# The chain of an RWKV scan on Trainium2: a second PSUM bank, products split by their output columns, one output addition, and I - X added in PSUM

## The chip, the cores and the metric

The kernel runs on one core of a Trainium2 chip. Its five engines work through instruction lists of their own, each in order: TensorE (PE, with the loads of its stationary operand shown apart as PEld), VectorE (DVE), ScalarE (ACT), GpSimd (POOL) and SyncE (SP, which issues the DMAs). They wait for each other through semaphores. The metric is the time of one execution on the device in microseconds (us); lower is better.

## The reference

The reference is one layer of a hybrid encoder on 1024 + 256 tokens of width 1024. The normalised input is projected to three branches, neighbourhood attention, a bidirectional RWKV-7 recurrence and attention to a memory; their gated outputs are merged, and a convolutional feed-forward layer follows. The change is in the recurrence, which has 8 heads of width 64 and runs once forward and once backward:

```
def step(s, inp):
    r_t, w_t, k_t, v_t, a_t, b_t = inp
    sa = einsum('bhij,bhj->bhi', s, a_t)
    s = s * w_t[:, :, None, :] + sa[..., None] * b_t[:, :, None, :] + v_t[..., None] * k_t[:, :, None, :]
    return s, einsum('bhij,bhj->bhi', s, r_t)
```

## The kernel before

The recurrence is computed in chunks of 64 tokens. One item of work is a pair of heads (p, 4 of them), a direction (d, 2) and a block of 256 tokens, that is 4 chunks (s, 5): 40 items and 160 chunks in all. `part_rwkv` goes through them, alternating the directions.

For each item `rw_prepare` (L538 on) makes what doesn't depend on the state. From loaded blocks it computes decays with small products into the tile `ps_l` (L558, L559), ScalarE, GpSimd and VectorE work, Gram products (`ps_gE` L608, `ps_gO` L611), masks (L618 to L623) and transposes (`ps_bt` L628, L631). Then it inverts a 128 x 128 triangular matrix per chunk: five levels of two products each (L653, L658) with copies on ScalarE (L655, L660), an addition and a transpose on VectorE (L661, L664) and masked copies on GpSimd (L650). The inverse X is refined once: L672 forms I - X on VectorE, L675 and L676 compute the product of the matrix (in two fp16 halves) with X, L678 adds both on VectorE, L681 multiplies by X again and L683 adds, which gives TT.

`rw_chain` carries the state from chunk to chunk. R holds, for each chunk and each of the two heads h, the state in 64 of its 128 partitions and the values V in the other 64. Per chunk: two products with L1 (L707, one for each head, 128 columns out of 128 partitions), a copy Q of both (L709, ScalarE), one product with TT (L710), two half copies back into R (L719 ScalarE, L720 VectorE), two products with L3 (L722), two additions that make the next chunk's state (L731, L732, VectorE) and two that make the output Ys (L733, L734, VectorE). GpSimd scales the state in between (L715, L717). All products of a chunk write one PSUM tile `ps_c`, of which there is one buffer.

TensorE is kept busy by other work: after each prepare and each chain `fill` puts in steps of the dense products of attention and gates (`ps_d`, L205), a fixed number per item. The written order is a request only: a scheduler at build time lays out every engine's list by priority and by its own estimate of costs, and the PSUM and SBUF buffers that are free in that estimate. The engines then follow these lists. PSUM has eight banks; a tile in one bank isn't written by TensorE and read by another engine at the same time, so accesses to one tile are ordered even where they touch different columns.

A matrix product has a shape of the array: 128 rows by 128 columns by default, 64*128 where the contraction is over 64 partitions (L608, L611, L628), 128*64 or 64*64 where it makes 64 output partitions. The profile shows it before the operand's shape. An fp32 product appears as two records.

Of the kernel before, what the change touches and what calls it, by code (L numbers as in the profile page):

```python
# [77 lines left out]
def make_consts():  # L78

    c = {}  # L80
    c["ident"] = np.eye(128, dtype=np.float32)
    c["ident16"] = np.eye(128, dtype=np.float16)
    hb = np.arange(128) // 64
    c["headones"] = (hb[:, None] == hb[None, :]).astype(np.float32)
# [70 lines left out]
class Builder:  # L155
# [195 lines left out]
    def rwkv_consts(self):  # L351
# [14 lines left out]
        self.reset = ld("reset", [128, 256])  # L366
        self.ident16 = ld("ident16", [128, 128], F16)
        d0 = ld("rw_decay0", [128, 2, 4])
        a0 = ld("rw_a0", [128, 2, 4])
# [134 lines left out]
    def part_rwkv(self):  # L504
        nc, tc = self.nc, self.tc
        with ExitStack() as cx:
            pool = cx.enter_context(self.pool("rw", 2))
            self.psg = cx.enter_context(self.pool("psg", 2, space=PSUM))
            self.psl = cx.enter_context(self.pool("psl", 1, space=PSUM))
            self.psi = cx.enter_context(self.pool("psi", 1, space=PSUM))  # L510
            self.psc = cx.enter_context(self.pool("psc", 1, space=PSUM))
            self.L1 = [pool.tile([128, 4, 2, 128], F32, name="L1_%d" % i, bufs=1) for i in range(3)]
# [25 lines left out]
    def rw_prepare(self, pool, p, d, s):  # L538
# [17 lines left out]
        nc.sync.dma_start(lw[dl], self.LW[s][dl])  # L556
        ps = self.psl.tile([128, 512], F32, tag="l", name="ps_l")
        nc.tensor.matmul(ps[:, 0:256], lhsT=self.decay2[dl, pc], rhs=lw[dl, 0], start=True, stop=True)  # L558
# [89 lines left out]
        for l in range(1, 6):  # L648
# [21 lines left out]
            X, XT = X2, XT2  # L670
        IX = tl([128, 4, 128], "IX", F16, bufs=1)
        nc.vector.tensor_sub(IX, bc(self.ident16), X)  # L672
        pe = self.psi.tile([128, 4, 128], F32, tag="i%d" % (i % 2), name="ps_e")
        for c in range(4):
            nc.tensor.matmul(pe[:, c, :], lhsT=Lh[:, c, :], rhs=X[:, c, :], start=True, stop=False)  # L675
            nc.tensor.matmul(pe[:, c, :], lhsT=Ll[:, c, :], rhs=X[:, c, :], start=False, stop=True)  # L676
        Er = IX
        nc.vector.tensor_add(f(Er), f(IX), f(pe))  # L678
        pe = self.psi.tile([128, 4, 128], F32, tag="i%d" % (i % 2), name="ps_n")
# [6 lines left out]
    def rw_chain(self, pool, it, state):  # L686
# [9 lines left out]
        for n, c in enumerate(order):  # L696
            if n == 0:
                if first:
                    nc.gpsimd.memset(R[0:64, c, 0, :], 0.0)
                    nc.gpsimd.memset(R[64:128, c, 1, :], 0.0)  # L700
                else:
                    S = state.pop((p, d))
                    nc.scalar.copy(R[0:64, c, 0, :], S[0:64])
                    nc.vector.tensor_copy(R[64:128, c, 1, :], S[64:128])
            ps = self.psc.tile([128, 3, 2, 64], F32, tag="c", name="ps_c")
            for h in range(2):
                nc.tensor.matmul(ps[:, 0, h, :], lhsT=L1[:, c, h, :], rhs=R[:, c, h, :], start=True, stop=True)  # L707
            Q = pool.tile([128, 2, 64], F32, tag="Q", name="Q", bufs=4)
            nc.scalar.copy(Q, ps[:, 0])  # L709
            nc.tensor.matmul(ps[:, 1].rearrange("p h i -> p (h i)"), lhsT=TT[:, c, :],  # L710
                             rhs=Q.rearrange("p h i -> p (h i)"), start=True, stop=True)
            more = n < 3 or not last
            if more:
                SW = pool.tile([128, 64], F32, tag="SW", name="SW", bufs=2)
                nc.gpsimd.tensor_scalar(SW[0:64], R[0:64, c, 0, :], scalar1=wC[0:64, c:c + 1], scalar2=1.0,  # L715
                                        op0=ALU.mult, op1=ALU.mult)
                nc.gpsimd.tensor_scalar(SW[64:128], R[64:128, c, 1, :], scalar1=wC[64:128, c:c + 1], scalar2=1.0,  # L717
                                        op0=ALU.mult, op1=ALU.mult)
            nc.scalar.copy(R[0:64, c, 0, :], ps[0:64, 1, 0, :])  # L719
            nc.vector.tensor_copy(R[64:128, c, 1, :], ps[64:128, 1, 1, :])  # L720
            for h in range(2):
                nc.tensor.matmul(ps[:, 2, h, :], lhsT=L3[:, c, h, :], rhs=R[:, c, h, :], start=True, stop=True)  # L722
            if more:
                if n < 3:
                    nx = R[:, order[n + 1]]
                    o0, o1 = nx[0:64, 0, :], nx[64:128, 1, :]
                else:
                    S = pool.tile([128, 64], F32, tag="S%d" % d, name="S", bufs=2)
                    o0, o1 = S[0:64], S[64:128]
                    state[(p, d)] = S  # L730
                nc.vector.tensor_add(o0, SW[0:64], ps[0:64, 2, 0, :])  # L731
                nc.vector.tensor_add(o1, SW[64:128], ps[64:128, 2, 1, :])  # L732
            nc.vector.tensor_add(Ys[64:128, c, :], Q[64:128, 0, :], ps[64:128, 2, 0, :])  # L733
            nc.vector.tensor_add(Ys[0:64, c, :], Q[0:64, 1, :], ps[0:64, 2, 1, :])  # L734
        nc.sync.dma_start(self.Y[d][p][:, 4 * s:4 * s + 4], Ys)
# [962 lines left out]
```

## Time and profile before

| | |
|---|---|
| runs, median (3) | 3095.74 us (3078.0 to 3098.25) |
| profiled execution | 3087.64 us |
| its span | 3085.9 us |
| mean granted clock of TensorE | 0.967 |
| the RWKV stage, first chain product to last | 391 to 1416 us of the span |

The span is the stretch between the first and the last instruction of the profiled execution; its own time is 1.7 us longer. The page divides the span into 40 slices; the RWKV stage is roughly slices 6 to 18. Busy times of TensorE include the time in which a product runs through the array, so a busy TensorE can still have room: how far apart the starts of successive records are says more.

### The profile page before, as it was taken

How to read it: one execution, taken by the hardware profiler on the slowest of the kernel's cores; microseconds unless marked ns; L12 is line 12 of the kernel's file. 1: busy time of each engine (PE TensorE's matmuls, PEld its weight loads, DVE VectorE, ACT ScalarE, POOL GpSimd, SP SyncE). 2: the span in 40 equal slices, each digit the busy share in tenths (PEclk: the TensorE clock that was granted, in tenths of full speed). 3: DMA queues.
4: the chain of work that ended last, by engine and by line, in shares of the span. 5: the costliest groups of instructions: out<-in, count | busy, mean ns of one | idle time of the engine just before them, and what ended most of it. 6: DMA issues, size and time to landing. Idle time of an engine off the chain costs nothing.

```text
span 3085.9 us, 49265 instructions
## 1 busy us (share of the span) xinstructions
PE 2929.3 (95%) x18164; PEld 2477.7 (80%) x18164; DVE 1946.3 (63%) x4001; ACT 1242.3 (40%) x2693; POOL 1082.5 (35%) x1186
## 2 busy tenths in 40 slices
PE   7999989999999998999989999999899999999999
PEld 6878867767777777777877788898799999997877
DVE  6233387887887888883435551474688888883233
ACT  6322344444444544552545551022244344343232
POOL 2000166765666766662122100000245544441100
PEclk9999988997999999999979999999999999999999
DMA  6332412221222222214546534544112222245343
GB/s 229 119 120 94 137 62 67 73 78 61 76 74 70 86 64 66 66 54 132 167 123 192 178 114 157 191 163 147 66 61 71 75 77 68 68 135 165 131 146 103
DMA packets 212743, 333.51 MB, mean 108 GB/s; under 512 B 45282, under 2 KB 109538, under 8 KB 212502
## 3 DMA queue, kind: packets, MB, share of 16 engines
q1 hardware_dynamic: 211062, 325.12, 32.6%
q10 hardware_dynamic: 1440, 5.24, 0.4%
q8 instruction: 143, 2.34, 0.3%
q14 instruction: 98, 0.80, 0.1%
HBM read 230.15 MB, written 104.07 MB: 108 GB/s over the span
## 4 chain that ended last, share of the span: by engine, by line
PE 75%; DVE 10%; POOL 6%; issue 3%; ACT 3%; DMA 2%; SPq 0%; ACTq 0%; POOLq 0%; DVEq 0%
PE ps_d L205 26%; PE ps_d L1470 16%; PE ps_d L1660 9%; PE ps_w L1167 3%; PE ps_o L945 3%; PE ps_c L722 2%; PE ps_c L707 2%; PE ps_y L653 1%; PE ps_gO L611 1%; PE ps_pt L863 1%; PE ps_x L658 1%; DVE X L661 1%; PE ps_gE L608 1%; PE ps_c L710 1%; PE ps_bt L628 1%
## 5 line engine op out<-in xcount | busy, mean ns | idle before, releaser
L205 PE MATMUL ps_d<-hT,whi 128*128 128x512 f32 (+1 forms) x2688 | 689.3, 381 | 3.5 <-ACT gt L824 2.9
L205 PEld LDWEIGHTS ps_d<-hT,whi 128*128 128x128 f32 x2688 | 450.5, 194 | 65.6 <-issue 5.8
L205 PE MATMUL ps_d<-hT,wlo 128*128 128x512 f32 (+1 forms) x1344 | 358.2, 383 | 0.0
L650 POOL TENSOR_TENSOR Lk<-Lh,c_lev 128x512 f16<-128x512 f16 x200 | 242.2, 1214 | 128.2 <-PE ps_y L653 127.0
L1660 PE MATMUL ps_d<-hT,h2T 128*128 128x512 f32 x1110 | 275.4, 394 | 7.3 <-POOL hT L183 4.1
L1660 PEld LDWEIGHTS ps_d<-hT,h2T 128*128 128x128 f32 x1110 | 210.5, 190 | 54.5 <-POOL hT L183 5.3
L205 PEld LDWEIGHTS ps_d<-hT,wlo 128*128 128x128 f32 x1344 | 229.6, 197 | 29.0 <-issue 2.8
L183 DVE TENSOR_TENSOR wlo<-wraw,whi 128x512 fp32r<-128x512 f32 x152 | 117.1, 781 | 192.9 <-ACT whi L182 192.0
L1374 DVE SCALAR_TENSOR_TENSOR xk<-xk,fconv,xk 128x642 f32<-128x642 f32 (+1 forms) x176 | 178.7, 1026 | 3.1
L655 ACT CAST Yl<-ps_y 128x512 f16<-128x512 f32 x200 | 116.8, 584 | 135.6 <-PE ps_y L653 134.8
L1470 PE MATMUL ps_d<-hT,fwx 128*128 128x256 f32 (+1 forms) x1080 | 159.0, 306 | 2.2 <-ACT fwx L182 1.6
L1470 PEld LDWEIGHTS ps_d<-hT,fwx 128*128 128x128 f32 x1080 | 156.5, 188 | 2.9 <-ACT fwx L182 1.9
L660 ACT CAST X<-ps_x 128x512 f16<-128x512 f32 x200 | 116.7, 584 | 101.7 <-PE ps_x L658 95.2
L1470 PE MATMUL ps_d<-hT,fw 128*128 128x256 f32 (+1 forms) x1032 | 156.1, 310 | 0.6 <-ACT hT L182 0.6
L1340 DVE TENSOR_TENSOR xk<-ps_d,xk 128x256 f32<-128x256 f32 (+1 forms) x308 | 140.6, 480 | 22.1 <-PE ps_d L1470 21.8
L1470 PEld LDWEIGHTS ps_d<-hT,fw 128*128 128x128 f32 x1032 | 153.2, 190 | 1.6 <-ACT hT L182 0.9
L1219 POOL TENSOR_TENSOR xk<-xk 128x1536 f32<-128x1536 f32 (+1 forms) x2 | 5.8, 2918 | 387.2 <-DVE xk L1157 387.2
L182 ACT CAST whi<-wraw 128x512 fp32r<-128x512 f32 x152 | 91.3, 620 | 119.9 <-PE ps_d L205 104.8
L205 PE MATMUL ps_d<-bo,whi 128*128 128x256 f32 (+2 forms) x640 | 127.0, 337 | 4.2 <-DMA bo<-O 3.1
L1383 ACT ACTIVATE xk<-xk 128x320 f32<-128x320 f32 (+1 forms) x88 | 41.7, 474 | 214.9 <-DVE xk L1387 139.8
L707 PEld LDWEIGHTS ps_c<-R,L 128*128 128x128 f32 x640 | 92.0, 201 | 43.2 <-issue 24.8
L1470 PE MATMUL ps_d<-h2T,fw 128*128 128x384 f32 (+1 forms) x840 | 125.4, 308 | 0.0
(353 smaller groups left out, 6437.6 us busy)
## 6 DMA issues: line engine op xcount, KB each, us to landing
wraw<-in_w_in SPq DMA_DIRECT2D x112, 256.0 KB, 2.9
wraw<-in_w_up SPq DMA_DIRECT2D x88, 256.0 KB, 2.6
kr<-RKV SPq DMA_DIRECT2D x40, 384.0 KB, 3.2
bo<-O SPq DMA_DIRECT2D x24, 640.0 KB, 8.7
gate<-GT SPq DMA_DIRECT2D x20, 640.0 KB, 4.0
h2T<-AD SPq DMA_DIRECT2D x17, 704.0 KB, 3.9
h2T<-AD SPq DMA_DIRECT2D x18, 640.0 KB, 5.1
draw<-in_w_down SPq DMA_DIRECT2D x44, 256.0 KB, 2.9
```

Of the source, the lines that this page charges most:

```text
L183: (eng or nc.vector).tensor_sub(lo, src, hi.bitcast(F32))
L205: nc.tensor.matmul(ps[:, :n], lhsT=w[:, k, :], rhs=x[k][:, t0:t0 + n], start=i == 0, stop=i == 3 * kt - 1)
L650: nc.gpsimd.tensor_mul(Lk, Lh, bc(self.lev[:, d, l, :]))
L655: nc.scalar.copy(Yl, py)
L660: nc.scalar.copy(f(X2), f(px))
L707: nc.tensor.matmul(ps[:, 0, h, :], lhsT=L1[:, c, h, :], rhs=R[:, c, h, :], start=True, stop=True)
L945: nc.tensor.matmul(o, lhsT=PT[0:h, j], rhs=V[0:h, k0 // 128 + j, f], start=j == 0, stop=j == nb - 1)
L1167: nc.tensor.matmul(ps[i][:, 512 * f:512 * f + 512], lhsT=self.merged(l, k, 128 * i, 128), rhs=r[:, 512 * f:512 * f + 512], start=k == 0 an ...
L1340: add = lambda o, y: nc.vector.tensor_add(o, ps, y)
L1374: nc.vector.scalar_tensor_tensor(o[:, :m], in0=z[j][:, lo + d:lo + d + m], scalar=fc[:, f + 22 * j, i:i + 1], in1=o[:, :m], op0=ALU.mult, ...
L1470: nc.tensor.matmul(ps, lhsT=w[:, u, 128 * k:128 * k + 128], rhs=B[c][j][v][:, k], start=n == 0, stop=n == 11)
L1660: nc.tensor.matmul(ps[n], lhsT=u, rhs=wd[f][:, v], start=f == 0 and m == 0, stop=f == 21 and m == 2)
```

## The change

`ps_c` gets two buffers. The bank for it comes from `ps_l`, whose own pool is removed and which now takes a buffer of the pool `psg` (2 buffers, shared with `ps_gE`, `ps_gO` and `ps_bt`).

The two L1 products of a chunk become four: for each head one that makes the 64 output partitions of the state half (K = 128) and one that makes the other 64 (K = 64, since the other rows are zero there). The product with TT then takes only the state half, 64 columns instead of 128. The two L3 products become four: the state halves (left out after the last chunk of a sequence) and the output halves. The output halves of both heads lie in one column block, so one addition over 128 partitions makes Ys. In the inversion the two terms of I - X are added in PSUM by two more fp16 products with identity matrices, and a ScalarE copy takes the result out in place of VectorE's subtraction and addition. The new constant -I in fp16 (32 KB) is loaded with the others.

```
-            self.psl = cx.enter_context(self.pool("psl", 1, space=PSUM))
...
-            self.psc = cx.enter_context(self.pool("psc", 1, space=PSUM))
+            self.psc = cx.enter_context(self.pool("psc", 2, space=PSUM))
...
-        ps = self.psl.tile([128, 512], F32, tag="l", name="ps_l")
+        ps = self.psg.tile([128, 512], F32, tag="g", name="ps_l")
...
-        IX = tl([128, 4, 128], "IX", F16, bufs=1)
-        nc.vector.tensor_sub(IX, bc(self.ident16), X)
...
-            nc.tensor.matmul(pe[:, c, :], lhsT=Lh[:, c, :], rhs=X[:, c, :], start=True, stop=False)
-            nc.tensor.matmul(pe[:, c, :], lhsT=Ll[:, c, :], rhs=X[:, c, :], start=False, stop=True)
-        Er = IX
-        nc.vector.tensor_add(f(Er), f(IX), f(pe))
+            for n, (l, r) in enumerate(((self.nident16, X[:, c]), (self.ident16, self.ident16), (Lh[:, c], X[:, c]),
+                                        (Ll[:, c], X[:, c]))):
+                nc.tensor.matmul(pe[:, c, :], lhsT=l, rhs=r, start=n == 0, stop=n == 3)
+        Er = tl([128, 4, 128], "IX", F16, bufs=1)
+        nc.scalar.copy(f(Er), f(pe))
...
-            ps = self.psc.tile([128, 3, 2, 64], F32, tag="c", name="ps_c")
-            for h in range(2):
-                nc.tensor.matmul(ps[:, 0, h, :], lhsT=L1[:, c, h, :], rhs=R[:, c, h, :], start=True, stop=True)
+            ps = self.psc.tile([128, 5, 64], F32, tag="c", name="ps_c")
+            lo, hi = slice(0, 64), slice(64, 128)
+            sides = ((0, lo, hi), (1, hi, lo))
+            for h, o, q in sides:
+                nc.tensor.matmul(ps[o, 0], lhsT=L1[:, c, h, o], rhs=R[:, c, h, :], start=True, stop=True)
+            for h, o, q in sides:
+                nc.tensor.matmul(ps[q, 1], lhsT=L1[o, c, h, q], rhs=R[o, c, h, :], start=True, stop=True)
...
-            nc.scalar.copy(Q, ps[:, 0])
-            nc.tensor.matmul(ps[:, 1].rearrange("p h i -> p (h i)"), lhsT=TT[:, c, :],
-                             rhs=Q.rearrange("p h i -> p (h i)"), start=True, stop=True)
+            nc.scalar.copy(Q, ps[:, 0:2])
+            nc.tensor.matmul(ps[:, 2], lhsT=TT[:, c, :], rhs=Q[:, 0], start=True, stop=True)
...
-            nc.scalar.copy(R[0:64, c, 0, :], ps[0:64, 1, 0, :])
-            nc.vector.tensor_copy(R[64:128, c, 1, :], ps[64:128, 1, 1, :])
-            for h in range(2):
-                nc.tensor.matmul(ps[:, 2, h, :], lhsT=L3[:, c, h, :], rhs=R[:, c, h, :], start=True, stop=True)
+            nc.scalar.copy(R[0:64, c, 0, :], ps[0:64, 2])
+            nc.vector.tensor_copy(R[64:128, c, 1, :], ps[64:128, 2])
+            for h, o, q in sides:
+                if more:
+                    nc.tensor.matmul(ps[o, 3], lhsT=L3[:, c, h, o], rhs=R[:, c, h, :], start=True, stop=True)
+            for h, o, q in sides:
+                nc.tensor.matmul(ps[q, 4], lhsT=L3[:, c, h, q], rhs=R[:, c, h, :], start=True, stop=True)
...
-                nc.vector.tensor_add(o0, SW[0:64], ps[0:64, 2, 0, :])
-                nc.vector.tensor_add(o1, SW[64:128], ps[64:128, 2, 1, :])
-            nc.vector.tensor_add(Ys[64:128, c, :], Q[64:128, 0, :], ps[64:128, 2, 0, :])
-            nc.vector.tensor_add(Ys[0:64, c, :], Q[0:64, 1, :], ps[0:64, 2, 1, :])
+                nc.vector.tensor_add(o0, SW[0:64], ps[0:64, 3])
+                nc.vector.tensor_add(o1, SW[64:128], ps[64:128, 3])
+            nc.vector.tensor_add(Ys[:, c, :], Q[:, 1], ps[:, 4])
```

With other buffers and other operations the scheduler lays out the lists of all engines anew. In the changed kernel the products are at L712 (L1, state halves), L714 (L1, other halves), L717 (TT), L729 (L3, state halves), L731 (L3, output halves) and L678 (the four products per chunk of the inversion); the additions are at L740, L741 (state) and L742 (Ys), and the dense products at L206.

Here is TensorE's list before, in the item before the last, from the third chunk's L3 products to the fourth chunk's TT product (a row may stand for several like instructions, x2 and so on; `ps_d` are the dense products):

```order
L722 MATMUL ps_c_15838<-R_15262,L3_15306 128x64 x2
L205 MATMUL ps_d_16070<-hT_75,wlo_16033 128x512 x3
L205 MATMUL ps_d_16070<-hT_75,whi_16032 128x512 x4
L707 MATMUL ps_c_15855<-R_15262,L1_2_3024 128x64 x2
L205 MATMUL ps_d_16070<-hT_75,whi_16032 128x512 x2
L710 MATMUL ps_c_15855<-Q_15858,TT_15454 128x128
```

And the same place in the changed kernel's list, to the fourth chunk's L1 products:

```order
L729 MATMUL ps_c_16551<-R_15945,L3_15989 64x64 x2
L731 MATMUL ps_c_16551<-R_15945,L3_15989 64x64 x2
L206 MATMUL ps_d_16768<-hT_75,wlo_16759 128x512 x2
L712 MATMUL ps_c_16571<-R_15945,L1_2_3023 64x64
L206 MATMUL ps_d_16768<-hT_75,wlo_16759 128x512
L712 MATMUL ps_c_16571<-R_15945,L1_2_3023 64x64
L714 MATMUL ps_c_16571<-R_15945,L1_2_3023 64x64 x2
```

Before, seven dense products stand between the last product of one chunk and the first of the next; now two stand before the first head's product and one more before the second head's.

On VectorE, the additions of a chunk before, in the middle of the stage:

```order
L683 TENSOR_TENSOR TT_9014<-XT0_8990,ps_n_9009 128x512
L731 TENSOR_TENSOR R_8502<-SW_9090,ps_c_9084 64x64
L732 TENSOR_TENSOR R_8502<-SW_9090,ps_c_9084 64x64
L733 TENSOR_TENSOR Ys_9047<-Q_9087,ps_c_9084 64x64
L734 TENSOR_TENSOR Ys_9047<-Q_9087,ps_c_9084 64x64
```

And now:

```order
L740 TENSOR_TENSOR R_8804<-SW_9424,ps_c_9416 64x64
L666 STREAM_TRANSPOSE XT0_9290<-X0_9287 128x512
L741 TENSOR_TENSOR R_8804<-SW_9424,ps_c_9416 64x64
L742 TENSOR_TENSOR Ys_9373<-Q_9421,ps_c_9416 128x64
L620 TENSOR_TENSOR LT_1_3025<-ps_gE_9508,c_tri_411 64x4x64
L621 TENSOR_TENSOR LT_1_3025<-ps_gO_9509,c_tri_411 64x4x64
```

Three additions per chunk are left of four. Before as now, other work (here a transpose) can stand between the first and the second.

In the two built lists of the stage, TensorE's array shape changes 504 times from one product to the next before and 1376 times now; changes between 128 and 64 rows are 504 of them before and 826 now, the rest are changes of columns alone.

## Rows read from the trace of the kernel before

**Rows 1.** The page's head: span, busy time of each engine, slices of TensorE, VectorE, clock.

```profile
span 3085.9 us, 49265 instructions
PE 2929.3 (95%) x18164; PEld 2477.7 (80%) x18164; DVE 1946.3 (63%) x4001; ACT 1242.3 (40%) x2693; POOL 1082.5 (35%) x1186
...
PE   7999989999999998999989999999899999999999
...
DVE  6233387887887888883435551474688888883233
```

**Rows 2.** Busy time of each engine in the stage (a window).

```profile
core 0: us, PE busy (x) PEld busy (x) DVE busy (x) ACT busy (x) POOL busy (x), PEclk, DMA share, GB/s
391.00:1416.00 1025.00, 951.55 (x6751) 744.09 (x6751) 840.71 (x1940) 493.59 (x1211) 653.14 (x863) 0.95 0.21 68
```

**Rows 3.** Chain of waits in the stage, share of it by engine and line.

```profile
by line: PE ps_d L205 21.5%; PE ps_c L722 5.8%; PE ps_c L707 5.6%; issue 5.4%; PE ps_y L653 3.9%; PE ps_gO L611 3.8%; PE ps_x L658 3.5%; DVE X L661 3.2%; PE ps_c L710 3.1%; PE ps_gE L608 3.0%; PE ps_bt L628 2.3%; DVE XT L664 2.1%; POOL Lk L
```

**Rows 4.** Waits in the stage: who waited for whom, us, times, longest.

```profile
ACT Q L709 <- PE ps_c L707: 112.1, 90, 3.7
...
DVE R L720 <- ACT R L719: 37.1, 50, 2.2
...
PEld ps_c L707 <- issue: 24.8, 44, 2.4
...
PE ps_c L707 <- DVE Ys L734: 12.3, 16, 2.1
...
ACT th L561 <- PE ps_l L559: 13.0, 18, 3.4
...
PEld L681 <- DVE IX L678: 7.2, 12, 1.8
...
PEld ps_c L707 <- DVE Ys L734: 4.2, 7, 1.1
```

**Rows 5.** TensorE, chunk products in the stage: records, busy us, mean ns, idle before.

```profile
L707 PE MATMUL ps_c<-R,L 128*128 128x64 f32 x640 | 105.1, 287 | 19.0 <-DVE Ys L734 12.3 <-issue 5.8 <-PE ps_gO L611 0.5
L722 PE MATMUL ps_c<-R,L 128*128 128x64 f32 x636 | 105.0, 288 | 17.1 <-DVE R L720 16.9
L710 PE MATMUL ps_c<-Q,TT 128*128 128x128 f32 x320 | 75.1, 318 | 1.4 <-ACT Q L709 1.3
```

**Rows 6.** Timeline of all engines, one chunk in the stage (start us, us).

```profile
674.84 0.61 PE L722 MATMUL ps_c<-R,L 128*128 128x64 f32 x4
...
675.38 0.93 PE L611 MATMUL ps_gO<-L,BK 64*128 64x128 f32 x6
675.49 0.21 DVE L731 TENSOR_TENSOR R<-SW,ps_c 64x64 f32<-64x64 f32 x1 [0.29 <-PE ps_c L722]
...
676.11 0.22 DVE L732 TENSOR_TENSOR R<-SW,ps_c 64x64 f32<-64x64 f32 x1
...
676.24 0.73 PE L205 MATMUL ps_d<-hT,whi 128*128 128x512 f32 x2
...
677.35 0.21 DVE L734 TENSOR_TENSOR Ys<-Q,ps_c 64x64 f32<-64x64 f32 x1
...
678.27 0.61 PE L707 MATMUL ps_c<-R,L 128*128 128x64 f32 x4
```

**Rows 7.** Timeline of TensorE after the stage: products of shape 64*64.

```profile
1528.36 0.56 PE L1058 MATMUL ps_yt<-c_ident,y 64*64 64x64 f32 x12
```

**Rows 8.** Timeline of TensorE before the stage: transposes of shape 128*64.

```profile
212.68 1.10 PE L205 MATMUL ps_d<-hT,whi 128*128 128x512 f32 x4
213.61 0.82 PE L495 MATMUL ps_vt<-c_ident,cvv 128*64 128x128 f32 x6
```

**Rows 9.** Timeline of TensorE: products of the refinement.

```profile
682.57 0.23 PE L675 MATMUL ps_e<-X,Lh 128*128 128x128 f16 x1
682.63 0.22 PE L676 MATMUL ps_e<-X,Ll 128*128 128x128 f16 x1
682.69 0.22 PE L675 MATMUL ps_e<-X,Lh 128*128 128x128 f16 x1
```

**Rows 10.** VectorE and ScalarE in the stage: records, busy us, mean ns, idle before.

```profile
L733 DVE TENSOR_TENSOR Ys<-Q,ps_c 64x64 f32<-64x64 f32 x159 | 35.4, 222 | 2.1 <-PE ps_c L722 0.9
L734 DVE TENSOR_TENSOR Ys<-Q,ps_c 64x64 f32<-64x64 f32 x159 | 33.7, 212 | 2.2
L678 DVE TENSOR_TENSOR IX<-IX,ps_e 128x512 f16<-128x512 f16 x40 | 27.3, 682 | 12.5 <-PE ps_e L676 11.9
L672 DVE TENSOR_TENSOR IX<-c_ident,X 128x512 f16<-128x512 f16 x40 | 23.6, 589 | 0.4
...
L669 ACT COPY XT<-ps_xt 128x512 f16<-128x512 f16 x40 | 23.4, 585 | 10.6 <-PE ps_xt L668 10.4
```

More of the change, by code (lines that the diff above doesn't have):

```diff
@@ L82, in make_consts @@
     c["ident16"] = np.eye(128, dtype=np.float16)
+    c["nident16"] = -c["ident16"]
     hb = np.arange(128) // 64
@@ L367, in rwkv_consts @@
         self.ident16 = ld("ident16", [128, 128], F16)
+        self.nident16 = ld("nident16", [128, 128], F16)
         d0 = ld("rw_decay0", [128, 2, 4])
@@ L508, in part_rwkv @@
             self.psg = cx.enter_context(self.pool("psg", 2, space=PSUM))
-            self.psl = cx.enter_context(self.pool("psl", 1, space=PSUM))
+            pass
             self.psi = cx.enter_context(self.pool("psi", 1, space=PSUM))
-            self.psc = cx.enter_context(self.pool("psc", 1, space=PSUM))
+            self.psc = cx.enter_context(self.pool("psc", 2, space=PSUM))
             self.L1 = [pool.tile([128, 4, 2, 128], F32, name="L1_%d" % i, bufs=1) for i in range(3)]
```

## The prediction

> **What bounds the kernel now.** I first read the page's head to see who is busy where. TensorE is busy for 95% of the span, but in the slices of the recurrence, the sixth to the eighteenth, VectorE is busy at seven to eight tenths, which it isn't in most of the rest [rows 1]. All that the change touches lies in this stage, so I cut it out as a window: 1025 us, with TensorE busy 952, VectorE 841 (82%), GpSimd 653, ScalarE 494, and a granted clock of 0.95 of full speed [rows 2]. Next I read the chain of waits of that window, because busy shares don't say who is waited for. It runs mostly through TensorE: dense products 21.5%, the chunk products L722 and L707 5.8% and 5.6%, so 117 us together, and no line of VectorE has more than 3.2% [rows 3]. The waits show the coupling: ScalarE's copy Q stood 112.1 us waiting for L707, but TensorE's lists wait for VectorE too, 16.5 us at L707 for the Ys additions (12.3 + 4.2) and another 24.8 us at L707 whose releaser isn't named [rows 4]. So this stage isn't held by one engine at its limit. TensorE, in list order, sets most of its pace, VectorE is close behind, and each us of either counts in part.
>
> How much of a TensorE us counts I take from the chunk products. Four records of L722 take 0.61 us, of which the last one's own run is 0.28, so they start 0.11 us apart [rows 5, 6]; 1276 records make 140 us, and 117 of these lie on the chain of waits [rows 3, 5]. I count 0.8 of what TensorE gains or loses in this stage.
>
> **The change part by part**, against the profiled execution's 3087.64 us, which is 8.1 us under the median of the runs.
>
> *The split products.* Now a chunk has 10 records at 0.11 us, 1.10 us. After it there are 16 records of half width, and two of L717 at 0.11, since that product loads the same 128 columns. No row shows an fp32 half product over 128 partitions. The nearest from below are the 64*64 products L1058, where two halves of the array overlap: twelve in 0.56 us, the last one's run some 0.22, so 0.03 us a record [rows 7]. From above it is the 128*64 transposes: six in 0.82 us, the last one's run some 0.27, 0.11 us a record, but these stream twice the columns [rows 8]. At 0.03 a chunk costs 16 x 0.031 + 0.22 = 0.72 us, a gain of 0.38 x 160 = 61 us, and 2 more for the L729 that 16 chunks leave out. At 0.11 everywhere a chunk would cost 1.98 us, a loss of 141. Between them, 0.055 where the two halves don't overlap but half the columns take half the time: 12 x 0.055 + 4 x 0.031 + 0.22 = 1.00, a gain of 16. I take the first, since the two halves lie in different columns like the pairs of L1058: 63 x 0.8 = **-50 us** (from -50 to +113).
>
> *Changes of the array's shape.* They cost something: L722's last record starts at 674.84 + 0.33 = 675.17 and L611, of 64 rows, starts at 675.38, 0.21 us later where 0.11 is usual; on the way back L611's last record starts near 676.03 and the next dense product at 676.24, again 0.21 [rows 6]. So a change between 128 and 64 rows costs 0.095 us. A change of columns alone seems free: L205's last record starts at about 213.38 and L495, with 64 columns, at 213.61, the 0.23 us by which the dense records stand apart anyway [rows 8]. The built lists have 322 more changes of rows: 322 x 0.095 = 31, x 0.8 = **+24 us**. The Trainium skill, TensorEngine Tiling (Array Packing), Tiling Modes, Key Properties, says that changing the tiling mode, not just the tile, drains TensorE, and it makes no exception for columns. By that rule all 872 more changes would cost, 83 us, x 0.8 = +66, which is a rival below; the trace bears out the rule for rows and not for L495, though that row uses only the left columns.
>
> *I - X in PSUM.* 320 more fp16 products, which start 0.06 us apart [rows 9]: 19 x 0.8 = **+15 us**. On VectorE L672 (23.6 us) and L678 (27.3) go; ScalarE gets 40 copies, priced at L669's 585 ns, 23 us in all on an engine that is busy for less than half of the stage [rows 2, 10]. The path through the refinement gets 8 products (0.48 us) longer and 0.1 us shorter by the copy, while 7.2 us of waits for L678 turn into waits for ScalarE [rows 4]. I put this at nothing: it is covered by the dense products, and at worst costs 40 x 0.4 = 16.
>
> *One Ys addition, two banks.* One of two additions of 0.21 to 0.22 us goes in each chunk, 34 us; with L672 and L678 VectorE loses 85 of 841 us [rows 2, 10]. What was waited for is the bank: the 16.5 us at L707 go [rows 4], **-16 us**. What is late next is the state itself: the next chunk's L712 reads R, which L740 and L741 write, and the second bank can't free that.
>
> *The new list.* Because the Ys additions no longer hold the bank, the scheduler puts L712 closer: the place shown has seven dense products (1.6 us at 0.23) between chunks before, and two (0.46 us) and three (0.69) before the first and second L712 now. What L712 needs is in the timeline: L722 ends at 675.45, the first state addition at 675.70 and the second, with another operation between them, at 676.33 [rows 6]. From the last product's start that is 0.53 us and 1.16 us. So the first half is short by 0.07 us and the second by up to 0.47; behind it TensorE's whole list stands, the inversion's products too. 144 chunks x 0 to 0.47, x 0.8, is 0 to 54 us; without that other operation the second would be ready too, so I take 0.15: **+17 us**.
>
> *Small ones.* `ps_l` in the shared pool has to wait for a buffer; it is read by two ScalarE operations early in a prepare. ScalarE's wait at L561 is 13.0 us in all now [rows 4]; 0 to as much again, I take 0. The extra 32 KB constant is loaded long before.
>
> Sum: -50 + 24 + 15 - 16 + 17 = -10 us, so 3078 beside this profile and **3086** beside the median.
>
> **The rivals.**
> - *VectorE sets the pace* (faster). For it: 82% busy, in order, and state additions that TensorE waits for. Against: no VectorE line over 3.2% of the chain of waits. Then 85 us x 0.82 = 70 us are saved and the TensorE terms hide: 3026.
> - *The halves don't overlap* (slower). The first term is then -13 instead of -50: +27, 3123, and 3250 if half the columns also save nothing.
> - *Every change of shape drains TensorE* (slower). 872 more changes x 0.095 x 0.8 = +66 in place of +24: +32, 3128. For it speaks that L712 and L731 use the right columns too, which L495 doesn't. Decided by whether the first record of L712 after a 128*128 product starts 0.09 us late.
> - *L712 waits behind VectorE* (slower). If other VectorE work regularly stands between L731's end and L741's, each chunk loses 0.47 us or more: +54 for +17, and the 16 us come back as waits for L741: +43, 3139. It decides once those additions end over 0.7 us after the last L731 starts.
> - *The bank frees nothing*: L712 stands where L707 stood, as the state is needed anyway. Then neither the 16 us nor the 17 us arise: -11, which is inside the forecast.
>
> **How the numbers follow.** About 1%, 31 us, is what a measurement of this kernel can tell from no change. Chances: forecast (with the last rival) 0.42, at 3086 with 3060 to 3115 by its small terms; VectorE 0.23; no overlap 0.14; all changes drain 0.12; L712 waits 0.09. Faster by over 1% means under 3065: most of VectorE's (0.21) and the low end of the forecast (0.09), 0.30. Slower by over 1% means over 3127: half of the two rivals just there (0.13) and L712 (0.08), 0.21, and 0.01 from the forecast's high end, 0.22. The rest, 0.48, is within 1%. For 8 in 10 I leave out a tenth at either end: from 3032, which cuts half of VectorE's case, to 3142.
>
> **What would show it.** In the profile after: records of L712, L729 and L731 in pairs, four in about 0.35 us, shows the first term right; 0.055 or 0.11 apart shows the rivals. The gap from a 128*128 product into L712, and out of L731, shows the price of a change of columns. The waits of L712 for L740 and L741 against 16.5 + 24.8 us at L707 show the list's term. VectorE should be busy for about 756 us in the stage. If the dense products alone take more of the stage's chain than now and the stage is shorter by over 40 us, VectorE was the pace. The prediction is wrong if the stage's length changes by much more than TensorE's records and these waits explain, since then the order of the whole list, which I priced at one place only, has done it.

## The result: 3.2% slower, and the profile after

The changed kernel takes 3196.26 us (median of 4 runs, 3173.67 to 3201.57), the kernel before 3095.27 in the same comparison: a ratio of 1.032, 95% interval [1.028, 1.036], some 101 us. I had forecast 3086, most likely within 1%, and 3032 to 3142 for eight cases in ten. The profiled execution took 3200.47 us. Its stage of the recurrence, first chain product to last, lasts from 398.7 to 1543.7, 1145 us against 1025 before; what lies ahead of it is 8 us longer and what follows it 15 us shorter. So the whole loss is in the stage that the change touches.

The window of the stage after, to be held against [rows 2]:

```profile
core 0: us, PE busy (x) PEld busy (x) DVE busy (x) ACT busy (x) POOL busy (x), PEclk, DMA share, GB/s
398.70:1543.70 1145.00, 1053.70 (x8278) 767.30 (x8277) 816.71 (x1702) 522.11 (x1254) 653.09 (x866) 0.91 0.19 61
```

Two things stand out. VectorE does 238 operations fewer and 24 us less work, and the stage is longer all the same, so VectorE's sum of work wasn't the pace. And the granted clock has fallen from 0.95 to 0.91: by the trace's record of the clock, 197 us of the stage run at half clock where 112 did. Half of such time is lost, 98 us against 56. TensorE's idle time has grown less, from 1025.00 - 951.55 = 73 us to 1145.00 - 1053.70 = 91.

TensorE's timeline (start us, us), one place in the middle of the stage; the L1 products of another chunk are at L712 and L714, the L3 products at L729 and L731:

```profile
902.26 0.40 PE L655 MATMUL ps_y<-X,Lk 128*128 128x128 f16 x4
902.59 0.34 PE L729 MATMUL ps_c<-R,L 128*64 128x64 f32 x4
902.75 0.29 PE L731 MATMUL ps_c<-R,L 128*64 128x64 f32 x4
902.97 0.74 PE L206 MATMUL ps_d<-hT,wlo 128*128 128x256 f32 x4
```

The halves overlap as the prediction said: four records in 902.75 - 902.59 = 0.16 us, 0.04 each, against 0.11 for L722 [rows 6]. But look at the two ends. A record of L655 runs 0.23 us, so the last one started at 902.66 - 0.23 = 902.43, and L729 follows 0.16 us later where these products stand 0.06 apart [rows 9]. The last L731 (0.24 us each) started at 903.04 - 0.24 = 902.80, and L206 follows 0.17 us later. Both are changes of columns alone, and each costs about 0.10 us. The block of eight half records takes 0.38 us from L729 to L206 and 0.10 to get into; unsplit its four records took 4 x 0.11 = 0.44. What the overlap gains, entering and leaving the shape takes.

The chunk products after, by form (busy us, mean ns, idle before), against [rows 5]:

```profile
L712 PE MATMUL ps_c<-R,L 128*64 128x64 f32 x640 | 90.4, 254 | 21.6 <-DVE R L740 21.5
...
L717 PE MATMUL ps_c<-Q,TT 128*128 128x64 f32 x320 | 62.4, 278 | 3.5 <-DVE TT L685 2.8 <-ACT Q L716 0.7
...
L714 PE MATMUL ps_c<-R,L 64*64 64x64 f32 x640 | 56.8, 253 | 0.0
L729 PE MATMUL ps_c<-R,L 128*64 128x64 f32 x576 | 53.4, 258 | 5.1 <-DVE R L726 5.0
L731 PE MATMUL ps_c<-R,L 128*64 128x64 f32 x640 | 51.6, 236 | 0.0
```

VectorE in the stage, by line (busy us, mean ns, idle before), against [rows 10]:

```profile
L663 DVE TENSOR_TENSOR X<-X,X 128x512 f16<-128x512 f16 x200 | 118.4, 592 | 65.8 <-ACT X L662 63.7
...
L742 DVE TENSOR_TENSOR Ys<-Q,ps_c 128x64 f32<-128x64 f32 x160 | 35.4, 221 | 8.1 <-PE ps_c L731 3.2
...
L646 DVE TENSOR_TENSOR XT<-XT,c_ident 128x512 f16<-128x512 f16 x40 | 34.2, 855 | 0.8
```

The Ys addition has halved, to 35 us, and L672 and L678 of [rows 10] are gone, 85 us in all, as forecast. But other operations have become slower, among them the inversion's additions L663 and L646. Before, at L661 and L644, they took 522 and 569 ns:

```profile
L661 DVE TENSOR_TENSOR X<-X,X 128x512 f16<-128x512 f16 x200 | 104.3, 522 | 22.5 <-ACT X L660 20.1
...
L644 DVE TENSOR_TENSOR XT<-XT,c_ident 128x512 f16<-128x512 f16 x40 | 22.8, 569 | 0.4
```

VectorE's work falls to 817 us instead of the 756 that I had forecast.

The waits of the stage (who waited for whom, us, times, longest), against [rows 4]:

```profile
ACT Q L716 <- PE ps_c L714: 74.6, 65, 3.0
...
PEld ps_c L712 <- DVE R L740: 31.8, 33, 2.1
PE ps_y L655 <- DVE X L663: 31.8, 34, 2.9
...
PE ps_c L712 <- DVE R L740: 21.5, 22, 1.7
...
PEld ps_c L712 <- issue: 8.1, 28, 0.7
...
PEld ps_c L712 <- DVE R L741: 6.7, 20, 0.5
```

L707 waited for the Ys additions, 16.5 us; for the Ys addition L742, L712 waits 1.6 us now. L712 waits for the state instead, 21.5 + 31.8 + 6.7 = 60 us on its two queues, and 8.1 for nothing named, 68 in all; L707 waited 12.3 + 4.2 for Ys and 24.8 + 5.8 for nothing named, 47 in all. The wait wasn't removed, it was handed on. The state isn't later than it was: the second addition ends 1.08 us at the median after the start of the last L731, where it ended 1.13 us after the last L722. It is L712 that stands closer behind: in the built lists two dense products lie between chunks at the median, where there were five. (L655's wait of 31.8 us for the inversion's additions was 19.3 us at L653 before.)

What can follow such a wait, in four successive windows of the changed kernel (the columns are those of the first window above):

```profile
595.00:600.00 5.00, 3.99 (x33) 2.88 (x34) 2.75 (x5) 3.22 (x9) 3.92 (x9) 1.00 0.00 0
600.00:602.00 2.00, 0.29 (x4) 0.09 (x2) 1.94 (x4) 0.50 (x1) 2.00 (x3) 1.00 0.35 131
602.00:608.90 6.90, 6.90 (x43) 5.88 (x43) 4.10 (x9) 1.53 (x5) 1.90 (x2) 0.51 0.19 57
608.90:618.00 9.10, 9.07 (x80) 7.05 (x76) 7.75 (x14) 5.36 (x13) 4.08 (x5) 1.00 0.34 103
```

and what ended the stall at 602 (timeline, PE and DVE):

```profile
601.73 0.21 DVE L740 TENSOR_TENSOR R<-SW,ps_c 64x64 f32<-64x64 f32 x1
...
601.99 0.73 PE L712 MATMUL ps_c<-R,L 128*64 128x64 f32 x4 [1.71 <-DVE R L740]
```

TensorE stands nearly idle for 2 us while L712 waits for L740, and right after it the clock is at half, 1.2 instead of 2.4 GHz, for 6.8 us in which TensorE is busy throughout. The stage has 24 such half-clock stretches, and 22 of them begin just before the end of a gap of 0.9 us or more between the starts of two of TensorE's records, or up to 3 us behind it, most often at the inversion's L655 (11) or at L712 (7). Before there were 14 stretches, 9 of them so placed. But such a gap alone doesn't do it: the stage has 58 of them, of which 22 are followed by half clock, and before it had nearly as many, 53, of which 9 were. So more half clock did not come with more gaps.

### The profile page after: what moved, and what is told of

The parts are those of the page before. It is cut to its first block, busy times and chain, and to the rows that moved or that the text cites. A ratio compares the mean times of both kernels' runs of the same rounds, so it can differ in the third digit from the quotient of the medians.

```text
span 3198.7 us, 52148 instructions
## 1 busy us (share of the span) xinstructions
PE 3029.0 (95%) x19700; PEld 2500.5 (78%) x19700; DVE 1928.6 (60%) x3761; ACT 1269.9 (40%) x2733; POOL 1081.0 (34%) x1186
## 4 chain that ended last, share of the span: by engine, by line
PE 77%; DVE 10%; POOL 6%; issue 3%; ACT 3%; DMA 1%; ACTq 0%; POOLq 0%; SPq 0%; DVEq 0%
PE ps_d L206 27%; PE ps_d L1478 16%; PE ps_d L1668 8%; PE ps_w L1175 3%; PE ps_o L953 3%; PE ps_c L712 2%; PE ps_y L655 1%; PE ps_gO L613 1%; DVE X L663 1%; PE ps_x L660 1%; PE ps_pt L871 1%; PE ps_gE L610 1%; POOL Lk L652 1%; PE ps_e L678 1%; PE ps_c L714 1%
## 5 line engine op out<-in xcount | busy, mean ns | idle before, releaser
L206 PE MATMUL ps_d<-hT,whi 128*128 128x512 f32 (+1 forms) x2688 | 714.0, 389 | 0.1
L206 PEld LDWEIGHTS ps_d<-hT,whi 128*128 128x128 f32 x2688 | 456.9, 197 | 72.1 <-issue 6.9
L206 PE MATMUL ps_d<-hT,wlo 128*128 128x512 f32 (+1 forms) x1344 | 363.7, 388 | 0.0
L206 PEld LDWEIGHTS ps_d<-hT,wlo 128*128 128x128 f32 x1344 | 231.6, 199 | 34.2 <-issue 1.0
L663 DVE TENSOR_TENSOR X<-X,X 128x512 f16<-128x512 f16 x200 | 118.4, 592 | 65.8 <-ACT X L662 63.7
L206 PE MATMUL ps_d<-bo,whi 128*128 128x256 f32 (+2 forms) x640 | 127.1, 337 | 3.9 <-DMA bo<-O 2.6
L655 PE MATMUL ps_y<-X,Lk 128*128 128x128 f16 x800 | 83.9, 229 | 46.6 <-DVE X L663 31.8
```

What stands on the lines that cost most here:

```text
L206: nc.tensor.matmul(ps[:, :n], lhsT=w[:, k, :], rhs=x[k][:, t0:t0 + n], start=i == 0, stop=i == 3 * kt - 1)
L655: nc.tensor.matmul(py[:, c, :], lhsT=Lk[:, c, :], rhs=X[:, c, :], start=True, stop=True)
L663: nc.vector.tensor_add(f(X2), f(X), f(X2))
```

## The experiments

Four theories stood at the beginning. **Theory 1:** every change of the array's shape costs, of columns too. **Theory 2:** the second bank, and the list that it lets the scheduler build, cost the time. **Theory 3:** the inversion's added products do. **Theory 4:** half clock is a loss of its own on top. "Changes of shape" are counted in the built list of the stage (498 before and 1371 after by this count, 504 and 1376 by the one ahead of the prediction). Every ratio is against the kernel before in the same comparison, with a 95% interval.

### The parts by themselves

s_only takes over the edits of `rw_chain` from the change's diff and none of the others; one `ps_c` bank:

```
+            ps = self.psc.tile([128, 5, 64], F32, tag="c", name="ps_c")
+            for h, o, q in sides:
+                nc.tensor.matmul(ps[o, 0], lhsT=L1[:, c, h, o], rhs=R[:, c, h, :], start=True, stop=True)
...
+            nc.vector.tensor_add(Ys[:, c, :], Q[:, 1], ps[:, 4])
```

> Only the split products and the single Ys addition; one ps_c bank, ps_l in its own pool and VectorE's I - X stay. The built list of TensorE's stage has 1248 changes of shape (498 before, 1371 with the whole change) and 4 dense products between chunks (median; 5 before, 2 with the whole change). Theory 1, every change of shape costs, of columns too, 0.093 us: 750 more changes are +70 us on TensorE, against -50 us for the overlapping halves, so it keeps most of the loss: +40 to +100 us, 3135 to 3195. Theory 2, the second bank and the list that it lets the scheduler build cost the time: no loss here, -40 to +20 us, 3055 to 3115. Theory 3, the inversion's added products cost it: likewise no loss here, 3055 to 3115.

Measured: 3165.57 us, 1.0246 [1.0216, 1.0275], +76 us.

b_only, the bank and `ps_l` in `psg`:

```
-            self.psl = cx.enter_context(self.pool("psl", 1, space=PSUM))
-            self.psc = cx.enter_context(self.pool("psc", 1, space=PSUM))
+            self.psc = cx.enter_context(self.pool("psc", 2, space=PSUM))
-        ps = self.psl.tile([128, 512], F32, tag="l", name="ps_l")
+        ps = self.psg.tile([128, 512], F32, tag="g", name="ps_l")
```

> Only the second ps_c bank, with ps_l in the pool psg; products, additions and inversion as before. 596 changes of shape instead of 498 and 3 dense products between chunks instead of 5. Theory 1 (changes of shape): 98 more changes are +9 us, so 3095 to 3115. Theory 2 (bank and list): most of the 101 us are here, 3140 to 3200. Theory 3 (inversion): no change, 3080 to 3110.

Measured: 3103.05 us, 1.0047 [1.0030, 1.0064], +14 us.

i_only, I - X in PSUM:

```
-        nc.vector.tensor_sub(IX, bc(self.ident16), X)
+            for n, (l, r) in enumerate(((self.nident16, X[:, c]), (self.ident16, self.ident16), (Lh[:, c], X[:, c]),
+                                        (Ll[:, c], X[:, c]))):
...
-        nc.vector.tensor_add(f(Er), f(IX), f(pe))
+        nc.scalar.copy(f(Er), f(pe))
```

> Only I - X added in PSUM; one bank, unsplit products. 320 more products of 0.06 us are 19 us on TensorE, 522 changes of shape, 4 dense products between chunks. Theory 1 and theory 2: +0 to +20 us, 3095 to 3115. Theory 3, the refinement lies on the one path that each item's inversion runs along and delays the next item by more than its products: +40 to +100 us, 3135 to 3195.

Measured: 3118.28 us, 1.0092 [1.0061, 1.0123], +28 us.

sb_only takes the edits of s_only and b_only together.

> Split products, single Ys addition and second bank, with VectorE's I - X. 1390 changes of shape, 2 to 3 dense products between chunks. Theory 1: the loss of the whole change or a little more, as it has the most changes of shape: 3160 to 3200, and at most 20 us above the split alone. Theory 2: as much as the bank alone, 3140 to 3200. Theory 3: no loss, 3055 to 3115.

Measured: 3186.54 us, 1.0304 [1.0267, 1.0340], +94 us. The whole change is at 1.032 and can't be told from it.

So three quarters of the loss come with the split alone, which speaks for theory 1 and leaves little to theories 2 and 3. But the two smaller edits lose more than their own terms would; that is taken up at the end.

### The price of a change of columns, by itself

The kernel before gets a small product of constants behind each L1 product, whose result isn't used, in three shapes. The list is the same for the first two:

```
+                nc.tensor.matmul(ps[:, 3, h, :], lhsT=self.ident16[:, :], rhs=self.ident16[:, 0:64], start=True, stop=True)
```

(d_full; in d_left the output rows and the columns of lhsT are 0:64, in d_right 64:128; `ps_c` gets the room.)

> The kernel before with a small fp16 product of constants behind each of the two L1 products of a chunk (320 in all, 64 columns of the moving operand, their result is not used), in the shape 128*128, so that no change of shape is added (524 against 498). 320 x 0.06 us = 19 us, +10 to +35 us against the kernel before: 3100 to 3125. It is the reference for the next two.

> The same products in the same list, but in the shape 128*64 on the left columns: 1136 changes of shape, 612 more than with 128*128, all of them of columns alone. Theory 1 (a change of columns costs 0.093 us wherever it is): 612 x 0.093 = 57 us more than the reference, 3155 to 3185. Theory of the prediction (a change of columns is free, as I read it from L495, which uses the left columns): as the reference, 3100 to 3125. Theory 4 (the clock gate gives half clock more often when the array is used in small pieces, and this is a loss of its own): more than 57 us above the reference, with clearly more half-clock time in the stage than the 112 us of before.

> The same on the right columns (1130 changes of shape; the built list differs by a few rows). Theory 1: as on the left, 3155 to 3185. Rival: only a move to the right columns drains, so the left costs nothing and this one 57 us.

Measured: d_full 3115.42 us, 1.0053 [1.0022, 1.0084]; d_left 3181.03, 1.0309 [1.0215, 1.0404]; d_right 3163.96, 1.0228 [1.0171, 1.0286]. By the medians the shape alone costs 66 us on the left and 49 on the right; over 612 and 606 changes that is 0.11 and 0.08 us each. Part of the 66 us is clock: of d_left's four runs two had a mean granted clock of 0.949 and 0.947, the other two 0.961, while d_full's ten had 0.962 to 0.970 and d_right's four 0.964 to 0.966. The two profiled executions are of nearly one clock, 3124.21 and 3167.79 us; the windows of their stages, d_full first:

```profile
394.00:1463.00 1069.00, 988.67 (x7062) 779.76 (x7061) 852.22 (x1941) 499.17 (x1211) 647.79 (x864) 0.92 0.20 65
```

```profile
390.00:1500.00 1110.00, 1048.34 (x7064) 815.46 (x7062) 847.62 (x1941) 500.03 (x1211) 645.32 (x864) 0.93 0.20 63
```

TensorE is busy for 60 us more, 0.10 us a change, and idle for 19 us less, so that the stage is 41 us longer: a change costs TensorE 0.10 us, and 0.07 of it reach the time. Two timelines of TensorE show the price directly. d_full:

```profile
907.20 0.41 PE L707 MATMUL ps_c<-R,L 128*128 128x64 f32 x2 [1.90 <-issue]
907.45 0.19 PE L708 MATMUL ps_c<-c_ident 128*128 128x64 f16 x1
907.47 0.41 PE L707 MATMUL ps_c<-R,L 128*128 128x64 f32 x2
907.72 0.19 PE L708 MATMUL ps_c<-c_ident 128*128 128x64 f16 x1
```

d_left:

```profile
913.94 0.43 PE L707 MATMUL ps_c<-R,L 128*128 128x64 f32 x2
914.31 0.22 PE L708 MATMUL ps_c<-c_ident 128*64 128x64 f16 x1
914.45 0.43 PE L707 MATMUL ps_c<-R,L 128*128 128x64 f32 x2
914.82 0.22 PE L708 MATMUL ps_c<-c_ident 128*64 128x64 f16 x1
```

Head to head takes 907.47 - 907.20 = 0.27 us without the change of shape and 914.45 - 913.94 = 0.51 with it: 0.12 us for going in and 0.12 for coming out, on the left columns. My reading that columns are free is refuted for such products, theory 1 is shown.

### Products on 64 rows beside products on 128

In s_k128 the L1 products of the other halves keep the shape of the state halves:

```
-                nc.tensor.matmul(ps[q, 1], lhsT=L1[o, c, h, q], rhs=R[o, c, h, :], start=True, stop=True)
+                nc.tensor.matmul(ps[q, 1], lhsT=L1[:, c, h, q], rhs=R[:, c, h, :], start=True, stop=True)
```

> The split products alone, as in the first experiment, but the L1 products of the other halves contract over all 128 rows instead of 64 (the added rows are zero), so that they have the shape of the state halves: 1088 changes of shape instead of 1248, same records, same number of dense products between chunks. Theory 1: 160 x 0.093 = 15 us less than the split alone, 3140 to 3160. Rival (what costs is the number of records and the waits, not the changes): no difference, 3158 to 3175. Theory 4: less by more than 15 us if fewer drains also leave less half-clock time.

Measured: 3111.70 us, 1.0070 [1.0040, 1.0101]: 54 us less than the split alone, with the same number of records. TensorE's timelines give 16 of them. s_only:

```profile
924.40 0.62 PE L205 MATMUL ps_d<-hT,wlo 128*128 128x256 f32 x3
924.95 0.34 PE L709 MATMUL ps_c<-R,L 128*64 128x64 f32 x4
925.21 0.33 PE L711 MATMUL ps_c<-R,L 64*64 64x64 f32 x4
925.48 0.39 PE L205 MATMUL ps_d<-hT,wlo 128*128 128x256 f32 x1
```

s_k128:

```profile
927.36 0.47 PE L205 MATMUL ps_d<-hT,whi 128*128 128x512 f32 x1
927.76 0.34 PE L709 MATMUL ps_c<-R,L 128*64 128x64 f32 x4
927.93 0.29 PE L711 MATMUL ps_c<-R,L 128*64 128x64 f32 x4
928.14 0.97 PE L205 MATMUL ps_d<-hT,whi 128*128 128x512 f32 x3
```

From L709 to L711 it is 0.26 us in the first and 0.17 in the second, so the change from 128*64 to 64*64 costs 0.09 to 0.10 us, 160 times. The rest shows in the clock. The windows of the two stages, s_only first:

```profile
390.00:1499.00 1109.00, 1021.36 (x7957) 745.62 (x7955) 834.04 (x1783) 496.62 (x1211) 648.53 (x864) 0.89 0.20 63
```

```profile
391.00:1454.00 1063.00, 969.82 (x7956) 713.00 (x7955) 835.53 (x1781) 493.39 (x1211) 649.29 (x864) 0.92 0.21 66
```

The stage is 46 us shorter, and its loss of clock falls from 1109 x 0.11 = 122 to 1063 x 0.08 = 85. The runs agree: the mean clocks of s_only's four are 0.946 to 0.954, those of s_k128's ten 0.959 to 0.968. So theory 4 holds here.

s_all64 asks whether it is the 64 rows or the change between shapes: all split products contract over 64 rows.

```
-                nc.tensor.matmul(ps[o, 0], lhsT=L1[:, c, h, o], rhs=R[:, c, h, :], start=True, stop=True)
+                nc.tensor.matmul(ps[o, 0], lhsT=L1[o, c, h, o], rhs=R[o, c, h, :], start=True, stop=True)
...
-                nc.tensor.matmul(ps[q, 4], lhsT=L3[:, c, h, q], rhs=R[:, c, h, :], start=True, stop=True)
+                nc.tensor.matmul(ps[q, 4], lhsT=L3[q, c, h, q], rhs=R[q, c, h, :], start=True, stop=True)
```

> The split products alone, with all of them, state halves and other halves of L1 and L3, contracted over only 64 rows (the rows of their own output half; the other rows' part of the sums is left out). All are then 64*64: 1105 changes of shape (1088 with all of them 128*64, 1248 in the split alone), the same number of records. If what the split alone lost over the all-128*64 version (54 us, of which 16 are 160 changes at 0.1 us) came from changes between 128*64 and 64*64, this one is as fast as the all-128*64 version: 3100 to 3125, half-clock time in the stage near 170 us. If products on half of the array's rows make the clock fall more often by themselves, it is slower: 3140 to 3190, half-clock time 240 us or more.

Measured: 3108.71 us, 1.0062 [1.0027, 1.0098], as fast as s_k128. Half of the rows is no loss by itself; mixing the two shapes is. (Its L1 products of the other halves and its L3 products of the state halves, not shown, take the same rows.)

after_k128 makes the edit of s_k128 in the whole change.

> The whole change, but the L1 products of the other halves contract over all 128 rows, so that they have the shape of the state halves: 1199 changes of shape instead of 1371, the list otherwise the same. If the 54 us that this edit gave the split alone are a matter of these changes and of the clock behind them, most of it comes back here: 3130 to 3165. If the second bank and the added products of the inversion hide it: 3180 to 3200.

Measured: 3166.63 us, 1.0237 [1.0183, 1.0290]: 30 us less than the whole change's median, 25 by the ratios, whose intervals just overlap. Its stage's window shows a clock of 0.94 where the whole change has 0.91; over the runs the means are 0.961 and 0.958, so how much of the 25 to 30 us is clock stays open.

### Smaller suspects, and the list

b_l is b_only without the second `ps_c` bank. one_ys leaves the products and has one Ys addition:

```
-            nc.vector.tensor_add(Ys[64:128, c, :], Q[64:128, 0, :], ps[64:128, 2, 0, :])
-            nc.vector.tensor_add(Ys[0:64, c, :], Q[0:64, 1, :], ps[0:64, 2, 1, :])
+            nc.vector.tensor_add(Ys[:, c, :], Q[:, 0, :], ps[:, 2, 0, :])
```

> The kernel before with ps_l in the pool psg and nothing else; one ps_c bank, the eighth bank unused. If the 14 us that the bank alone cost come from the shared pool (gE, gO and bt wait for ps_l's reads or it for theirs): 3100 to 3115. If they come from the list that the second ps_c bank brings: 3080 to 3100.

> The kernel before with one Ys addition over 128 partitions in place of the two over 64 (it adds the first head's columns for both, so half of Ys is not what the reference has); everything else as before, 536 changes of shape instead of 498, 4 dense products between chunks instead of 5. The prediction's term for it was -16 us (16.5 us in which TensorE waited at L707 for the Ys additions): 3075 to 3087. If VectorE set the pace of the stage, its 34 us would count nearly in full: 3060 to 3075. If those waits only pass to the next one (the state additions, which the next chunk's products need anyway): no change or the few us of the 38 more changes of shape, 3090 to 3110.

Measured: b_l 3115.01 us, 1.0064 [1.0025, 1.0102]; one_ys 3108.51, 1.0087 [1.0042, 1.0132]. Taking 34 us of work from VectorE made the kernel 22 us slower. That lies in the range for waits that only pass on, at its upper end, and 38 more changes of shape (4 us) don't explain it. What all these edits share is that the scheduler writes new lists, so the next runs do the same work in another list: n_heads swaps the order of the heads in the L1 products, n_fill takes FILL_ALL 0.965 for 0.955 (which moves some dense products into the stage as well), and the last two swap the heads in the split kernels.

```
-            for h in range(2):
+            for h in (1, 0):
                 nc.tensor.matmul(ps[:, 0, h, :], lhsT=L1[:, c, h, :], rhs=R[:, c, h, :], start=True, stop=True)
...
-            sides = ((0, lo, hi), (1, hi, lo))
+            sides = ((1, hi, lo), (0, lo, hi))
```

> The kernel before with the two L1 products of a chunk written in the other order of heads: the same work, but all five engines' lists come out otherwise from there on (520 changes of shape against 498). If a new list alone costs what the small edits cost, because the list of before is a good one: +10 to +25 us, 3100 to 3120. If lists are alike on the average and each edit's cost is its own: within 8 us of the kernel before, 3085 to 3103.

> The kernel before with FILL_ALL 0.965 instead of 0.955, one hundredth more dense steps in the stage: the same work, another list (504 changes of shape). The same two expectations: 3100 to 3120 if a new list alone costs, 3085 to 3103 if not.

> The split products in one shape (as s_k128), with the order of heads swapped: same work, another list, 1112 changes of shape against 1088. The changes are worth 2 us. If lists scatter by 10 to 20 us either way: 3095 to 3135. If not: 3108 to 3118.

> The whole change with the order of heads swapped: same work, another list, 1255 changes of shape instead of 1371 (the second bank leads the scheduler to part fewer pairs). 116 x 0.1 = 12 us of changes, and half-clock time with them: 3165 to 3190. If the list of the changed kernel were an unlucky one and the split itself nearly free: 3140 or less. If lists scatter little and the changes weigh little: 3190 to 3200.

Measured: n_heads 3103.90 us, 1.0041 [1.0013, 1.0068]; n_fill 3112.50, 1.0085 [1.0056, 1.0114]; s_k128_heads 3110.42, 1.0042 [1.0001, 1.0084]; after_heads 3179.57, 1.0280 [1.0229, 1.0331]. The same work in another list was 13 and 26 us slower in the two trials: it seems that the list of the kernel before is a good one, and that an edit pays for losing it. With that, b_only, b_l, one_ys, d_full and the split in one shape show no loss that could be told from a new list's, and i_only little, if any. The list of the changed kernel isn't an unlucky one, as far as one other tells: that one, with 116 changes of shape fewer, gives 3180, and the two intervals overlap.

No kernel here is faster than the one before.

## Why the prediction was wrong

- **Which step failed:** "A change of columns alone seems free", read from L495 [rows 8]. The row was read rightly, but it is a row of another operation: line 495 is a transpose (`nc.tensor.transpose`), and I let it decide the cheaper of two prices for 550 changes of products, against rows that showed 0.095 us for every change of rows [rows 6]. d_left against d_full shows 0.10 us of TensorE's time for a change of columns. The rival "every change of shape drains TensorE" was right for the products, and so was the page behind it, the Trainium skill, TensorEngine Tiling (Array Packing), Tiling Modes, Key Properties: the trace agrees with it, at about 0.10 us a change, of rows or of columns. For such transposes to 64 columns the trace of before shows no price on either side. Behind L495 of [rows 8]:

```profile
213.61 1.04 PE L495 MATMUL ps_vt<-c_ident,cvv 128*64 128x128 f32 x8
214.41 2.78 PE L205 MATMUL ps_d<-hT,whi 128*128 128x512 f32 x11
```

The last L495 starts at 213.61 + 1.04 - 0.27 = 214.38, and L205 follows 0.03 us later; behind the 128*64 product of d_left the next one takes 0.14. All 24 changes between L495 and L205 at full clock look like this, in and out. (Transposes of 64 rows, L628, do pay: L205 follows them after 0.15 us.) Why those to 64 columns are free hasn't been tried.
- **The split products:** the overlap is there, 0.04 us a record against the 0.031 that I took, so a chunk's products would gain 1.10 - (16 x 0.04 + 0.22) = 0.24 us, not 0.38. But a chunk gets in and out of the shape twice, 4 x 0.10 = 0.40 us. s_k128 and its second list, 13 to 22 us above the kernel before, can't be told from a new list alone: in one shape the split is worth about nothing.
- **The 64*64 products:** a fifth change in each chunk, between 128*64 and 64*64. I counted it as a change of rows at 0.095 us, which was its direct price; that the granted clock would be lower with it was in no term. Undoing it gave 54 us in the split alone, and 25 to 30 in the whole change, there at the edge of the noise.
- **The clock:** the prediction read 0.95 as a property of the stage. It went to 0.91, and 98 - 56 = 42 us more are lost at half clock in the profiled execution, about a third of the stage's 120. The windows around 602 us show one such fall: a stall of 2 us is followed by 6.8 at half clock. The four kernels that mix 128*64 and 64*64 (s_only, sb_only, the whole change and after_heads) have mean clocks of 0.950 to 0.958 over their runs, the four whose split products keep one shape (s_k128, s_k128_heads, s_all64, after_k128) 0.960 to 0.964. Why mixing does that, with waits and records alike, stays open.
- **One Ys addition, two banks (-16):** not there. one_ys shows no gain, and after the change L712 waits 68 us where L707 waited 47. "The bank frees nothing" was right on the bank. "L712 waits behind VectorE" was right on the wait: those additions end over 0.7 us after the last L731 starts in 143 of 144 cases, as the rival asked, and the 60 us for the state are near its price of 54.
- **The new list (+17):** about right at the place shown (21 us more of waits at L712 than at L707), but the price of a new list isn't only there. It was the sentence on being wrong that named it: two new lists of the same work cost 13 and 26 us.
- **I - X in PSUM (+15) and VectorE:** i_only's 28 us less a new list leave 2 to 15. VectorE's 24 us less busy time bought nothing, and one_ys's 34 us nothing that shows above a new list, which speaks against the rival in which it sets the pace.

With 0.10 us for all 872 more changes the sum would have been -10 - 24 + 872 x 0.10 x 0.8 = +36, 3132. With the overlap as measured (+17) and no gain from the bank (+16) it is +69, 3165, and the clock's 42 us make 111. The two profiled executions are 113 us apart. That is an estimate from terms that lean on each other, with the prediction's 0.8 in it, and no run divides the loss so; the slower additions have no term in it.

## What to carry to other kernels

Count the changes of the array's shape in the built list before splitting a product: a split into column halves pays only if what it saves between entering and leaving is more than the two changes cost (0.2 us here, about two unsplit records). Keep split neighbours in one shape, even if half of the rows are zeros. Take a price from a row of the same operation: the transpose L495 was no measure for a product. And where a scheduler writes the lists, time the same work in another list first; here that alone was worth 0.4 to 0.9%.

## What the runs showed of the hardware

- A change of the array's shape from one product to the next costs 0.09 to 0.12 us of TensorE's time, of rows, of columns, and between 128*64 and 64*64; on left and right columns 0.07 to 0.08 of it reach the kernel's time. The transposes L495, shown by the profile as 128*64, cost nothing on either side (L205 follows after 0.03 us).
- fp32 half products in different columns overlap: four half records take 0.16 us, where four whole ones take 0.44 for twice the work.
- VectorE's additions of two fp16 tiles in SBUF go with what GpSimd does meanwhile. Of the 200 at L661 before, the 77 beside an idle GpSimd (under a tenth of their time overlapped) took 420 ns on the mean, the 55 beside a busy one (over nine tenths) 619; of the 200 at L663 after it is 75 at 424 and 49 at 801. They lie on each inversion's path. Why they got slower still in the changed kernel wasn't tried.
- A stall of TensorE of about 2 us can be followed by 3 to 20 us at half clock; of the stage's 58 gaps of 0.9 us or more, 22 were followed by half clock, before 9 of 53. The kernel before shows what this is worth: in one comparison its runs go from 3067.09 us at a mean granted clock of 0.975 to 3107.90 at 0.957.
